# A pooling mixer with two-level fast products: output weights kept as split pairs in memory, and a second-level product for one more block

## The chip, the cores and the metric

The kernel runs on one core of one Trainium2 chip. The metric is the device time of one execution, in microseconds (us). The engines that matter are TensorE (matrix products; PE in the profile, its weight loads PEld), VectorE (DVE), ScalarE (ACT), GpSimd (POOL) and the DMA queues, which are fed by SyncE (SP) and by GpSimd.

## The reference

With DEPTH = 1 only the pooling mixer runs. For x of 4096 frames by 1024 channels, in float32:

```python
normed = rms_norm(x, norm_w)
u, gate = split(normed @ in_w, 2)              # in_w: 1024 x 2048
pooled = trailing_mean(u, 2 / 4 / 8 / 16 by channel group) - u
mixed = einsum('bsgc,gcd->bsgd', pooled, group_w) + group_b
y = mixed * scale * silu(gate)
h = x + y @ out_w                              # out_w: 1024 x 1024
out = rms_norm(h, final_norm_w)
```

## The kernel before, in words

Each product of matrices is computed in float32 precision from float32r operands: a value is stored as a high part (a copy to float32r on ScalarE) and a low part (value minus high part, a subtraction on VectorE), and a product is the sum of three matmuls, high times high, high times low and low times high (`mm3`, line 794). Writing the two parts is called splitting (`split`, line 203).

On top of this, products are made by a fast scheme with seven products P1 to P7 of half-size blocks in place of eight (a Strassen-Winograd scheme). Both sides need sums of their blocks first. In some places one of the seven is itself computed by seven smaller ones, which the code calls inner products.

The steps are a list, executed by one loop (line 1894 on): four input blocks of 1024 frames for the first side ("a", blocks a0 to a3), four for the second side ("b", b0 to b3; the gate and the rest of the pooled channels), each with the seven products in the order P1, P2, P7, P6, P5, P4, P3; then eight output blocks of 512 frames ("o", o0 to o7) in the order P1, P7, P6, P2, P5, P4, P3. A product of an input block is 48 matmuls of 512 columns, one of an output block 24. In b1 to b3 P7 is an inner product of 84 matmuls of 256 columns (`product_seven`, line 733). In the output blocks:

- o0: all seven products plain.
- o1: P2 as seven inner leaves of 6 matmuls of 256 columns each (`product_inner`, line 970; `leaf`, line 933). The leaves P2, P4, P1, P3, P7 run in the place of P2, the leaf P6 within the product P5, between its two rows, and the leaf P5 after it.
- o2 to o7: P2 as in o1 and P7 as an inner product as well, in an order written out by hand (`steady`, line 1511; from two steps ahead of o2 each engine's instructions keep the order of the program, class `InOrder`, line 65).

Up to there the order on each engine is chosen by the framework's scheduler, which goes by the order of the program and by when it thinks that an instruction's inputs are ready. `tc.issue_after(x)` puts instructions behind x on x's engine.

The inner product P2 needs sums of the four quarters of the weight's blocks (`sum_inner`, line 841, from two raw halves read by `load_inner`, line 836) and their splits (`split_weight`, line 864), which live in three of the `st` buffers ("kept") and in a quarter of P2's own weight tile, so the plain P2 can't be used once they are formed. In the kernel before they are formed during o0 and o1 (the table `forming`, line 1877). The operand's sums are made by `split_inner` (line 882), whose second half (`rest`, line 898) runs at the step P6. `add_inner` (line 981) adds a PSUM bank of the inner product into the rows of the output on VectorE; the leaf P6 writes a bank that the first of these additions reads.

Output weights: `load_wo` and `make_wo` (lines 376 and 381) run in b1 and b2 at P7 and P6, one half of out_w each: the rows are scaled on ScalarE, the sums of the blocks made on VectorE (`combine`, line 290), and the seven results stored to memory as float32 by SP's queue (`store_weights`, line 303; tensors `wod`). In b3 `load_w` (line 387) reads each back into a buffer on SP's queue, half by half (512 KB), and splits it into the weight tile `w`, as soon as the input side has used that tile for the last time.

Buffers: 11 tiles `st` and 8 tiles `vt` of 4 KB a partition, handed out in order of age (class `Slots`, line 37); a load into a buffer waits until its last user is done. Four tiles `op` hold split operands in turn (`next_op`, line 546). The pooled and gated result y is stored to memory (`yd`, function `pool`, line 1052) and read back by the output blocks. The residual x is added into the output rows by GpSimd's DMA (`add_h`, line 1162).

Of the kernel before, what the change touches and what calls it, by code (L numbers as in the profile page):

```python
# [15 lines left out]
P = 128  # L16
# [70 lines left out]
def kernel(  # L87
# [115 lines left out]
    def split(dst, src):  # L203
# [14 lines left out]
    t3d = [dram.tile([P, 2, H], F32, name=f"t3d{h}") for h in range(2)]  # L218
    wod = {
        i: [dram.tile([P, 2, H], F32, name=f"wod{i}_{h}") for h in range(2)]  # L220
        for i in range(P1, P7 + 1)
    }
    sd = [
        {
# [78 lines left out]
    def store_weights(dst, h, b11, b21, b12, b22):  # L303
        sync.dma_start(out=dst[P1][h], in_=b11)
        sync.dma_start(out=dst[P2][h], in_=b21)
        for i, u in combine(b11, b21, b12, b22).items():
            sync.dma_start(out=dst[i][h], in_=u)
            give(u)


# [75 lines left out]

    def load_w(src, i):
        for h in range(2):
            u = take()
            sync.dma_start(out=u, in_=src[i][h])  # L390
            with tc.issue_after(evicted[0]):
                split(w[i][h], u)
            give(u)
# [482 lines left out]
    def end_weights(i):  # L876
        for u in raws.pop(i)["held"]:
            give(u)
# [306 lines left out]

    def split_o(b, i):
        s = oxs[b]
        if i == P2 and b >= OWN - 1:
            return split_inner(s["12"])
        t = next_op("p (s a b) -> p s a b", s=2, a=4)  # L1190
        if i == P7:
            s["3"] = take("p (a b) -> p a b", a=4)
            sub(s["3"], s["11"], s["21"])
        elif i == P6:
            add(s["21"], s["21"], s["22"])
            sub(s["11"], s["21"], s["11"])
# [668 lines left out]
    def row_plan(b):  # L1865
# [8 lines left out]
        )  # L1874

    scales, summed = {}, []
    forming = {
        (0, P4): lambda: load_inner(P2),
        (0, P3): lambda: sum_inner(P2),
        (1, P1): lambda: split_weight(P2, P7, P6),  # L1880
        (1, P7): lambda: (split_weight(P2, P5, P4), end_weights(P2), load_inner(P7)),
        (1, P6): lambda: sum_inner(P7),
        (1, P4): lambda: (split_weight(P7, P7, P6, P5, P3), keep_temps(P7)),
    }
    forming_seven = (P7, P6, P5, P4)

    for n in range(2, len(steps)):
# [15 lines left out]
            for j in rows.get(i, ()):  # L1903
                load_row(b + 1, j // 4, j % 4, early if b == 0 and i == P7 else None)
        if kind == "o":
            while len(gathered) < (6 if b else 3 * (i in (P4, P3))) and st.free and len(st.free) + len(vt.free) > 4:
                gathered.append(st.keep())
                kept.append(gathered[-1])
# [8 lines left out]
        if kind == "o" and (b, i) in forming:  # L1917
            with tc.issue_after(latest_split[0]), tc.issue_after(latest_copy[0]):
                forming[b, i]()
        if n >= own_from - 2:  # L1920
            InOrder.on = n == own_from - 2 or InOrder.on
            steady(n)
# [44 lines left out]
        if kind in ("a", "b"):  # L1967
# [1 line left out]
            if kind == "a":  # L1969
                pool_due(n)  # L1970
            if kind == "b" and b == NB - 1:
                for p in {P1: (), P2: (), P7: (P1,), P6: (P2, P7), P5: (P6, P5)}.get(i, (i,)):
                    load_w(wod, p)
            if kind == "b" and b in (1, 2) and i == P7:
                load_wo(b - 1)
# [61 lines left out]
```

## Time and profile before

| | |
|---|---|
| median of 3 runs | 907.41 us (906.5 to 909.38) |
| profiled execution | 907.14 us, span of its instructions 905.3 us |
| TensorE busy | 894.6 us (99%), 4554 matmuls |
| VectorE busy | 736.8 us (81%) |
| ScalarE busy | 518.6 us (57%) |
| GpSimd busy | 147.3 us (16%) |
| granted TensorE clock | 0.998 of full speed |
| DMA | 203.30 MB, mean 225 GB/s |

How to read the lines below: a group of instructions is given by engine, operation, the tile written, the tiles read and their shapes, then the count, busy time in us and the mean duration of one in ns, then the idle time of the engine just before them with what ended it. In lists in order of time the first number is the start and the second the duration, both in us, with the idle time before it and its releaser in brackets. Nearly all elementwise work has the line L79, that of the recording helper, so one goes by tiles. L799 is the plain product (`mm3`), L941 the leaves of the inner P2 and of the inner P7 in the output blocks, L745 the inner P7 of the input blocks. A matmul's duration overlaps the next one's, so what a matmul costs is read from the distance of starts in a long stream. By the chain, P7 of b1 starts at 417.60 us; the plain products of o0 begin at 612.0 us.

### The profile page before, as it was taken

What the parts mean: (1) busy time and instruction counts of PE and PEld (TensorE: products, weight loads), DVE (VectorE), ACT (ScalarE), POOL (GpSimd) and SP (SyncE); (2) the same over time, 40 slices, a digit from 0 to 9 for tenths busy, and PEclk for the clock granted to TensorE, in tenths of its full rate; (3) what the DMA queues carried; (4) which work ended last, traced back from release to release, by engine and by line L of the source; (5) the groups of instructions that cost most, each with busy time, mean ns of one, the idle gap of its engine ahead of it and who ended that gap; (6) DMA issues with size and microseconds to landing.
All of it is one profiled execution on the core that took longest, in us unless ns stands there. A gap on an engine that the chain in (4) does not pass through costs nothing.

```text
span 905.3 us, 12421 instructions
## 1 busy us (share of the span) xinstructions
PE 894.6 (99%) x4554; PEld 791.7 (87%) x4554; DVE 736.8 (81%) x910; ACT 518.6 (57%) x848; POOL 147.3 (16%) x244
## 2 busy tenths in 40 slices
PE   9999999999999999999999999999999999999996
PEld 7888888888888888889889889888889898998996
DVE  3899896984996997694596497699898878888798
ACT  7869547446445465346545644855557466565464
POOL 0031110110111000100010011011132343342430
PEclk9999999999999999999999999999999999999999
DMA  9989779677769565245574574756673855945953
GB/s 339 402 313 320 263 279 314 219 299 286 270 248 363 180 236 183 94 163 190 212 244 175 202 262 142 269 188 204 206 220 81 221 176 142 240 143 138 264 179 116
DMA packets 77756, 203.30 MB, mean 225 GB/s; under 512 B 7296, under 2 KB 25088, under 8 KB 77696
## 3 DMA queue, kind: packets, MB, share of 16 engines
q1 hardware_dynamic: 57872, 143.77, 46.0%
q0 software_dynamic: 19104, 57.69, 20.7%
q10 hardware_dynamic: 720, 1.06, 0.3%
q8 instruction: 35, 0.57, 0.3%
q14 instruction: 25, 0.20, 0.1%
HBM read 130.13 MB, written 72.36 MB: 224 GB/s over the span
## 4 chain that ended last, share of the span: by engine, by line
PE 50%; DVE 21%; DMA 10%; issue 6%; ACT 3%; POOL 1%; SPq 0%; DVEq 0%; POOLq 0%; ACTq 0%
PE bank L799 44%; DVE vt L79 8%; DVE st L79 6%; DVE op L79 5%; PE bank L745 3%; DMA vt<-yd 3%; PE bank L941 3%; DMA st<-wvd 2%; ACT op L79 1%; DMA st<-yd 1%; DVE w L79 1%; DMA out<-vt 1%; ACT vt L79 1%; DMA st<-wod 1%; DMA vt<-rd 1%
## 5 line engine op out<-in xcount | busy, mean ns | idle before, releaser
L799 PE MATMUL bank<-op,w 128*128 128x512 f32 x2544 | 550.6, 379 | 0.2 <-ACT st L79 0.2
L799 PEld LDWEIGHTS bank<-op,w 128*128 128x128 f32 x2544 | 480.4, 189 | 68.9 <-ACT st L79 0.6
L799 PE MATMUL bank<-w,op 128*128 128x512 f32 (+1 forms) x1044 | 230.5, 377 | 0.0
L799 PEld LDWEIGHTS bank<-w,op 128*128 128x128 f32 x1044 | 192.3, 189 | 25.0
L79 DVE TENSOR_TENSOR op<-st,op 128x1024 fp32r<-128x1024 f32 x120 | 145.9, 1220 | 60.1 <-ACT op L79 59.7
L79 ACT ACTIVATE op<-st 128x1024 fp32r<-128x1024 f32 x120 | 125.8, 1052 | 86.4 <-PE bank L799 31.2
L79 ACT ACTIVATE op<-vt 128x1024 fp32r<-128x1024 f32 x65 | 68.3, 1053 | 63.0 <-DVE vt L79 40.6
L79 ACT ACTIVATE vt<-bank 128x512 f32<-128x512 f32 (+1 forms) x122 | 67.4, 577 | 43.9 <-PE bank L799 37.8
L79 DVE TENSOR_TENSOR op<-vt,op 128x1024 fp32r<-128x1024 f32 x65 | 78.4, 1218 | 14.2 <-ACT op L79 14.1
L79 DVE TENSOR_TENSOR st<-st,st 128x1024 f32<-128x1024 f32 (+1 forms) x47 | 51.3, 1104 | 31.6 <-ACT st L79 16.8
L79 ACT ACTIVATE bank<-bank 128x512 f32<-128x512 f32 (+1 forms) x84 | 41.1, 490 | 53.1 <-PE bank L799 39.5
L79 POOL COPY vt<-tails 128x32 f32<-128x32 f32 x14 | 17.0, 1219 | 301.4 <-ACT tails L79 130.3
L79 ACT ACTIVATE st<-bank 128x512 f32<-128x512 f32 (+1 forms) x62 | 35.6, 588 | 37.5 <-PE bank L799 22.7
L79 DVE TENSOR_TENSOR vt<-bank,vt 128x512 f32<-128x512 f32 (+1 forms) x90 | 51.3, 596 | 6.0 <-PE bank L941 4.6
L79 ACT ACTIVATE st<-st 128x1024 f32<-128x1024 f32 x34 | 35.8, 1055 | 28.6 <-DVE st L79 27.1
L79 DVE TENSOR_TENSOR st<-bank,st 128x512 f32<-128x512 f32 (+1 forms) x72 | 43.7, 622 | 6.0 <-PE bank L941 3.1
L79 POOL DMA_DIRECT2D sd<-st x45 | 24.0, 535 | 125.1 <-DVE st L79 77.9
L941 PEld LDWEIGHTS bank<-w,op 128*128 128x128 f32 x312 | 40.4, 191 | 1.7
L79 DVE TENSOR_TENSOR st<-st,vt 128x1024 f32<-128x1024 f32 (+1 forms) x34 | 39.1, 1168 | 2.7 <-DMA vt<-rd 2.4
L941 PE MATMUL bank<-w,op 128*128 128x256 f32 x312 | 41.1, 275 | 0.0
L79 DVE TENSOR_TENSOR vt<-vt 128x1024 f32<-128x1024 f32 (+3 forms) x43 | 38.2, 890 | 0.2
L79 DVE TENSOR_TENSOR_SCAN vt<-vt,window 128x1040 f32<-128x1040 f32 x16 | 37.7, 2374 | 0.6 <-DMA wod<-vt 0.5
(118 smaller groups left out, 768.5 us busy)
## 6 DMA issues: line engine op xcount, KB each, us to landing
sd<-st POOLq DMA_DIRECT2D x45, 512.0 KB, 4.2
st<-sd SPq DMA_DIRECT2D x42, 512.0 KB, 4.0
st<-in_xt SPq DMA_DIRECT2D x28, 512.0 KB, 7.4
st<-in_x SPq DMA_DIRECT2D x21, 512.0 KB, 7.9
yd<-st SPq DMA_DIRECT2D x20, 512.0 KB, 3.3
vt<-yd SPq DMA_DIRECT2D x17, 512.0 KB, 10.5
st<-wod SPq DMA_DIRECT2D x16, 512.0 KB, 5.1
out<-vt POOLq DMA_DIRECT2D x16, 512.0 KB, 3.5
```

The source lines that it names most:

```text
L79: r = f(*args, **kwargs)
L745: latest[0] = nc.tensor.matmul(cell(n, c).rearrange("p (a s) -> p a s", s=2), x1, x2, start=i == P1 and k + m == 0, stop=k == 1 and m == 2 ...
L799: latest[0] = nc.tensor.matmul(ps, a, b, start=start and n == 0, stop=stop and n == 2, skip_group_check=True).ins
L941: latest[0] = nc.tensor.matmul(ps, x1, x2, start=start and k + n == 0, stop=k == 1 and n == 2, skip_group_check=True,).ins
```

## The change

The sums for P5, P4 and P3 of the output weights are split where they are made, in b1 and b2: `store_weights` copies the high part into a second buffer, subtracts it, and stores both to new tensors `pair...` by SP's queue. In b3 (P5 and P4 at the steps P4 and P3, P3 at P3) `load_w` reads each half of a pair, 1 MB, straight into the weight tile by GpSimd's queue, with no buffer and no split. P1, P2, P6 and P7 are loaded and split as before.

P2 of o0 becomes an inner product like that of o1. Its weights are therefore formed earlier: loaded at P2 of b3, summed at P7, three `st` buffers taken at P6, split at P5 and P4. The weights of the inner P7 are formed in o1 as before.

```diff
     wod = {
         i: [dram.tile([P, 2, H], F32, name=f"wod{i}_{h}") for h in range(2)]
-        for i in range(P1, P7 + 1)
+        for i in (P1, P2, P6, P7)
+    }
+    pairs_d = {
+        i: [dram.tile([P, 2, 2, H], F32, name=f"pair{i}_{h}") for h in range(2)]
+        for i in (P5, P4, P3)
     }
...
         for i, u in combine(b11, b21, b12, b22).items():
-            sync.dma_start(out=dst[i][h], in_=u)
+            if i in dst:
+                sync.dma_start(out=dst[i][h], in_=u)
+            else:
+                high = take()
+                latest_copy[0] = copy(high.bitcast(F32R), u).ins
+                latest_split[0] = sub(u.bitcast(F32R), u, high).ins
+                for v, t in enumerate((high, u)):
+                    sync.dma_start(out=pairs_d[i][h][:, v], in_=t)
+                give(high)
             give(u)
...
     def load_w(src, i):
         for h in range(2):
+            if i not in src:
+                gpsimd.dma_start(out=w[i][h], in_=pairs_d[i][h].bitcast(F32R))
+                continue
             u = take()
             sync.dma_start(out=u, in_=src[i][h])
...
     def split_o(b, i):
         s = oxs[b]
-        if i == P2 and b >= OWN - 1:
+        if i == P2:
             return split_inner(s["12"])
...
+    def gather(count):
+        for _ in range(count):
+            gathered.append(st.keep())
+            kept.append(gathered[-1])
+
     forming = {
-        (0, P4): lambda: load_inner(P2),
-        (0, P3): lambda: sum_inner(P2),
-        (1, P1): lambda: split_weight(P2, P7, P6),
-        (1, P7): lambda: (split_weight(P2, P5, P4), end_weights(P2), load_inner(P7)),
-        (1, P6): lambda: sum_inner(P7),
-        (1, P4): lambda: (split_weight(P7, P7, P6, P5, P3), keep_temps(P7)),
+        ("b", NB - 1, P2): lambda: load_inner(P2),
+        ("b", NB - 1, P7): lambda: sum_inner(P2),
+        ("b", NB - 1, P6): lambda: gather(3),
+        ("b", NB - 1, P5): lambda: split_weight(P2, P7, P6),
+        ("b", NB - 1, P4): lambda: (split_weight(P2, P5, P4), end_weights(P2)),
+        ("o", 1, P7): lambda: load_inner(P7),
+        ("o", 1, P6): lambda: sum_inner(P7),
+        ("o", 1, P4): lambda: (split_weight(P7, P7, P6, P5, P3), keep_temps(P7)),
     }
...
-                for p in {P1: (), P2: (), P7: (P1,), P6: (P2, P7), P5: (P6, P5)}.get(i, (i,)):
+                for p in {P1: (), P2: (), P7: (P1,), P6: (P2, P7), P5: (P6,), P4: (P5,), P3: (P4, P3)}[i]:
                     load_w(wod, p)
```

More of the change, by code (lines that the diff above doesn't have):

```diff
@@ L1905 @@
         if kind == "o":
-            while len(gathered) < (6 if b else 3 * (i in (P4, P3))) and st.free and len(st.free) + len(vt.free) > 4:
-                gathered.append(st.keep())
-                kept.append(gathered[-1])
+            while b and len(gathered) < 6 and st.free and len(st.free) + len(vt.free) > 4:
+                gather(1)
             if b > 0 or i in (P4, P3):
@@ L1916 @@
             advance("split", n, split_step, split_reach)
-        if kind == "o" and (b, i) in forming:
+        if (kind, b, i) in forming:
             with tc.issue_after(latest_split[0]), tc.issue_after(latest_copy[0]):
-                forming[b, i]()
+                forming[kind, b, i]()
         if n >= own_from - 2:
```

## The prediction

> **What bounds the kernel now.** I read the busy times first, then the time cut into stages, then the chain that ended last, and then, around the one place where TensorE stops, its instructions and VectorE's in order of time. The page's head:
>
> ```profile
> span 905.3 us, 12421 instructions
> PE 894.6 (99%) x4554; PEld 791.7 (87%) x4554; DVE 736.8 (81%) x910; ACT 518.6 (57%) x848; POOL 147.3 (16%) x244
> ```
>
> TensorE lacks 10.7 us of the span. The table by stages says where (start:end; TensorE, weight loads, VectorE, ScalarE, GpSimd busy with their counts; granted clock; DMA share; GB/s):
>
> ```profile
> 660.00:670.00 10.00, 9.91 (x61) 8.76 (x59) 9.93 (x14) 8.20 (x13) 4.34 (x6) 1.00 0.86 239
> 670.00:680.00 10.00, 8.31 (x44) 7.49 (x45) 9.99 (x18) 2.42 (x4) 1.77 (x2) 1.00 0.96 252
> 850.00:906.00 56.00, 48.01 (x278) 43.42 (x276) 46.86 (x93) 27.40 (x59) 11.62 (x19) 0.96 0.54 167
> ```
>
> Some 8 us are the last stage, 56.00 less 48.01, of which 0.7 lie past the end; the change touches nothing there. Between 660 and 680 are 0.09 + 1.69 us, the only gap that the change can close; the rest is the start. So it can gain only by issuing less TensorE work or by closing that gap. The gap, in order of time on TensorE:
>
> ```profile
> 612.01 51.96 PE L799 MATMUL bank<-w,op 128*128 128x512 f32 x240
> 667.16 2.76 PE L799 MATMUL bank<-w,op 128*128 128x512 f32 x12
> 671.69 0.94 PE L941 MATMUL bank<-inner,op 128*128 128x256 f32 x6 [1.77 <-DVE vt L79]
> ```
>
> The 240 are ten products of 24: all seven of output block 0 (612.0 to 648.4) and three of block 1. At 671.69 the inner product P6 of block 1 starts 1.77 us late. Its bank is read first by an addition on VectorE, which in the order of its queue stands behind this:
>
> ```profile
> 666.29 0.68 DVE L79 TENSOR_TENSOR vt<-vt 128x512 f32<-128x512 f32 x1
> 667.01 1.42 DVE L79 TENSOR_TENSOR vt<-vt,vt 128x512 f32<-128x512 f32 x2
> 668.94 2.35 DVE L79 TENSOR_TENSOR op<-vt,op 128x1024 fp32r<-128x1024 f32 x2
> 671.22 0.42 DVE L79 TENSOR_TENSOR vt<-bank,vt 128x256 f32<-128x256 f32 x1
> ```
>
> VectorE is simply behind there. How long it has been shows in the stages:
>
> ```profile
> 443.00:486.00 43.00, 43.00 (x201) 37.65 (x200) 42.42 (x46) 18.04 (x26) 3.69 (x4) 1.00 0.65 225
> 514.00:558.00 44.00, 44.00 (x206) 38.53 (x205) 41.75 (x44) 18.90 (x27) 4.50 (x3) 1.00 0.60 210
> 587.00:640.00 53.00, 53.00 (x247) 46.43 (x246) 52.83 (x53) 26.15 (x34) 9.39 (x8) 1.00 0.69 210
> 640.00:671.00 31.00, 29.91 (x154) 26.27 (x152) 27.46 (x36) 22.47 (x42) 8.95 (x20) 1.00 0.58 183
> ```
>
> From 587 to 640 it is busy 52.83 of 53 us, from 640 to 671 27.46 of 31.
>
> **The change, part by part.** First TensorE. Block 0's P2 loses 24 matmuls of 512 columns and gets seven leaves of 6 of 256 columns, 42. Both kinds stand in the chain in undisturbed streams:
>
> ```profile
> 427.20 62.16 PE bank L799 x288
> ...
> 701.29 3.35 PE bank L941 x30
> ```
>
> 62.16/288 = 0.2158 us and 3.35/30 = 0.1117 us. 24 x 0.2158 = 5.18 less 42 x 0.1117 = 4.69: 0.49 us gained, with no cover, since TensorE is the bound. The Trainium skill (TensorE: Matmul & The Clock Gate, Back-to-back issue gap) speaks against it: it gives 131 ns for a sustained 512-column matmul and 81 ns for 128 columns, since the weight load has its share; about halfway in columns, an estimate of 97 ns for 256, the swap would cost 42 x 97 - 24 x 131 ns = 0.9 us. The rows here show 216 and 112 ns, so the measurement decides.
>
> Then the elementwise work that moves:
>
> ```profile
> L79 DVE TENSOR_TENSOR w<-st,w 128x1024 fp32r<-128x1024 f32 x25 | 29.6, 1218 | 5.5 <-ACT w L79 5.5
> L79 ACT ACTIVATE w<-st 128x1024 fp32r<-128x1024 f32 x25 | 25.5, 1054 | 6.0 <-DVE st L79 2.4 <-DMA st<-wod 2.1 <-PE bank L799 1.4
> L79 DVE TENSOR_TENSOR inner<-vt,inner 128x512 fp32r<-128x512 f32 x6 | 3.9, 679 | 0.0
> L79 ACT ACTIVATE inner<-vt 128x512 fp32r<-128x512 f32 x6 | 3.6, 633 | 0.0
> L79 DVE TENSOR_TENSOR vt<-bank,vt 128x256 f32<-128x256 f32 x29 | 11.4, 416 | 4.7 <-PE bank L941 4.6
> ```
>
> Splits of P5, P4, P3: six copies of 1.05 and six subtractions of 1.22 us leave input block 3 and the start of output block 0 (7.3 us of VectorE, 6.3 of ScalarE) and go, three each, to P6/P5 of input blocks 1 and 2 of the second side: 3.7 us of VectorE and 3.2 of ScalarE in each. VectorE is full after both (42.42 of 43, 41.75 of 44), so all behind them comes later. What waits is the split of operands, four tiles ahead of TensorE:
>
> ```profile
> 443.13 1.23 DVE L79 TENSOR_TENSOR st<-st,st 128x1024 f32<-128x1024 f32 x1 [8.39 <-ACT st L79]
> 451.21 1.21 DVE L79 TENSOR_TENSOR op<-st,op 128x1024 fp32r<-128x1024 f32 x1
> 452.34 1.21 DVE L79 TENSOR_TENSOR op<-vt,op 128x1024 fp32r<-128x1024 f32 x1
> 447.96 1.06 ACT L79 ACTIVATE op<-vt 128x1024 fp32r<-128x1024 f32 x1 [2.97 <-PE bank L799]
> ```
>
> The copy at 447.96 waits for the tile that P5 has just left, so it fills the fourth tile ahead, and the subtraction at 451.21 belongs to the third: P3's first half. With 48 matmuls a product (10.36 us) from 427.20, P3 starts at 458.3, the subtraction ends at 452.4: 5.9 us of cover. Starts 1.13 us apart make the three added ones 3.4 us, so 2.5 are left. Cost nothing; without the cover 3.4 us in each block. The same holds for the three stores more in SP's queue of each block (seven become ten): loads of later operands stand behind them and come up to 3.4 us later, plus 1.5 MB of traffic at 225 GB/s, 7 us at the very worst; I take none of it, and both ends go to the range.
>
> What is left of this backlog reaches the inner P7 of block 3, where cover is thin:
>
> ```profile
> 560.46 0.17 DVE L79 TENSOR_REDUCE window<-vt 128x1 f32<-128x16 f32 x1 [2.43 <-POOL vt L79]
> 562.74 1.23 DVE L79 TENSOR_TENSOR op<-st,op 128x1024 fp32r<-128x1024 f32 x1 [0.98 <-ACT op L79]
> 564.31 0.83 PE L745 MATMUL bank<-op,w 128*128 128x256 f32 x6
> ```
>
> The subtraction at 562.74 ends at 564.0 and feeds the matmuls of 564.31. Of 3.4 us late, 2.43 and 0.98 go into these two waits if they shrink; if the first is passed on (GpSimd waits there for a store that itself follows VectorE), about 0.8 us are lost. I take none.
>
> Inner weights of P2: four half-size sums and four splits of 0.68 us (5.4 us of VectorE, 2.5 of ScalarE) and two loads of 512 KB move from output blocks 0 and 1 to P2 to P4 of input block 3. New for block 0: four sums of about 0.42 (1.7), a second split (1.22 and 1.05), six additions of 0.42 (2.5): 5.4 us of VectorE. Balance from 587 on: -7.3 + 2.7 (the splits of the weights; the sums fall before) + 2.9 = -1.7 by block 0's P2; the additions bring +2.5, and 5.4 are gone after 640: some 4.6 us less before 671. That is more than the 1.77 of the gap. But GpSimd's read-and-add of x into these rows moves one product later in block 0, its squares later still, and ScalarE waits for them in order: up to 3 us come back. I take 1.5 of the 1.78 as gained; bounds 0 and 1.78.
>
> The loads of P5, P4, P3 become six of 1 MB on GpSimd's queue, without a buffer in between. Each waits until TensorE has left that half of the old weights (586.1, 591.3, 596.5, 601.6, 606.8, 612.0, half a product apart), and GpSimd's copies of window history and its adds of x are queued behind. They are due at P5 (632.8), P4 (638.0) and P3 (643.2). DMA has room then:
>
> ```profile
> 604.00:619.00 15.00, 15.00 (x71) 13.12 (x71) 15.00 (x13) 9.08 (x13) 0.00 (x0) 1.00 0.15 57
> 624.00:641.00 17.00, 17.00 (x81) 14.88 (x80) 16.13 (x16) 5.34 (x8) 4.02 (x5) 1.00 1.08 302
> ...
> sd<-st POOLq DMA_DIRECT2D x45, 512.0 KB, 4.2
> ...
> st<-in_x POOLq DMA_DIRECT2D x18, 256.0 KB, 7.5
> ```
>
> No row shows 1 MB, nor a load that writes float32r. By the plain store it is at most 2 x 4.2 = 8.4 us; by the adding load 4 x 7.5 = 30 us. I take the plain one, as these only move data. One after another from 586.1 the last lands at 636.5, 7 us ahead: cost nothing.
>
> **Sum.** -0.49 - 1.5 = -2.0 us. The profiled execution took 907.14 us around its span of 905.3, and the median of the three is 907.41, so it stands 0.27 lower. 907.14 - 2.0 = 905.2 us (0.24% under the median). The most that all terms can give is -0.49 - 1.78: 904.9.
>
> **The rivals.**
> Slow pair loads (slower). If a megabyte on GpSimd's queue takes over (643.2 + 1.3 - 586.1)/6 = 9.7 us, P3's second half is late, and from there each us costs six: at 12 us it lands at 658, 14 us late, 919 us. For it: the adding load's 7.5 us for a quarter of the size. Against: that one was measured where DMA was full (1.08), these run where it is 0.15. The Trainium skill (DMA: Bandwidth & Descriptors, SWDGE vs HWDGE vs iDMA) says that a DMA into float32r always casts and must be issued from GpSimd; no run here shows what such a cast takes.
>
> Buffers (slower). Two buffers hold P2's halves and three its sums through input block 3, 5 of 19 (11 + 8). SP gets loads off at the pace at which buffers come free:
>
> ```profile
> 571.26 1.41 SPq L79 DMA_DIRECT2D st<-sd  x2
> 583.96 8.92 SPq L79 DMA_DIRECT2D st<-wod  x6
> ```
>
> 8.92/6 = 1.5 us each, so five fewer are 7.4 us late loads. Operands loaded at 571.26 serve products from 591.3 on, which covers that; from about 12 us on TensorE waits, and each further us counts: 3 to 6 us, 908 to 911. Against: six loads for splits take no buffer any more.
>
> The gap stays, or moves to block 0, where the same bank now has the same reader: 907.14 - 0.49 = 906.7, with both 908.4. For it: VectorE is full there as well; against: the balance above.
>
> The backlog at block 3's P7: 905.2 + 0.8 = 906.0.
>
> Short matmuls paced by their weight loads: from 5.18/42 = 0.123 us each the swap loses; at 0.146 it is 1 us worse than nothing, 906.6. The row of 0.1117 speaks against it. It is the rule of the skill's page named above.
>
> **How the numbers follow.** Covers hold: 0.55, 905.2, by its own range 904.5 to 906.5. Gap stays or moves: 0.14. Backlog: 0.05. Matmul pace: 0.03. Buffers: 0.11. Slow pair loads: 0.12. What this kernel's measurement can tell from no change is about 0.3%, 2.7 us: under 904.7 or over 910.1. Faster by more needs the likeliest case with all of its terms and a little luck: 0.17 of its 0.55. Slower: buffers and pair loads, 0.23. The rest, 0.60, is within. The range runs from 904.2 to 912.0; outside are most of the slow pair loads, the far end of the buffers and a little below.
>
> **What would show it.** Right: 42 more short and 24 fewer long matmuls; no idle TensorE near 670; VectorE with idle time between 612 and 671; six 1 MB loads landing under 9.7 us each, and the copies of P3's weights gone from ScalarE near 613. Wrong: TensorE waiting for a DMA into w in block 0, for a split in input blocks 1 to 3, or for an addition from a bank near 633.

## The result and the profile after

The changed kernel takes 929.49 us (median of 4 runs, 927.58 to 930.88) against 906.95 for the kernel before in the same session: a ratio of 1.0235 (95% interval 1.0213 to 1.0257). It is 2.35% slower; 905.2 was predicted, with 912.0 as the upper end. Of the runs further down, one of the four of held_late took 4430 us and is left out of its median.

The profiled execution took 927.58 us. Its head, with busy times by engine:

```profile
span 925.8 us, 12489 instructions
...
PE 902.2 (97%) x4572; PEld 797.3 (86%) x4572; DVE 743.0 (80%) x921; ACT 518.5 (56%) x849; POOL 150.0 (16%) x250
```

The span grew by 20.5 us in two parts. TensorE's idle time is 925.8 - 902.2 = 23.6 us, where it was 10.7: 12.9 more. And TensorE is busy 7.6 us longer, though its work shrank by the 0.49 us of the swap (4572 matmuls, 18 more, as 42 less 24 say). The idle part, in order of time on TensorE (start, duration, what runs, and in brackets the wait before it with its releaser; lines are 15 further down than before, so L814, L956 and L760 are the former L799, L941 and L745):

```profile
470.24 2.00 PE L814 MATMUL bank<-op,w 128*128 128x512 f32 x8 [1.22 <-DVE op L79]
475.06 22.04 PE L814 MATMUL bank<-op,w 128*128 128x512 f32 x87 [2.82 <-DVE op L79]
576.38 1.37 PE L760 MATMUL bank<-op,inner 128*128 128x256 f32 x6 [4.84 <-ACT st L79]
641.90 2.86 PE L814 MATMUL bank<-w,op 128*128 128x512 f32 x12 [2.31 <-ACT bank L79]
652.17 3.92 PE L814 MATMUL bank<-w,op 128*128 128x512 f32 x10 [3.63 <-DVE op L79]
```

The gap near 670 is gone, as predicted. In its place are five waits, 14.82 us together, at three places: the first product of b2 (1.22 + 2.82), the inner P7 of b3 (4.84), and o0 at its P6 and P5 (2.31, 3.63).

The longer busy time has its row in the table by stages (start:end; length, TensorE, weight loads, VectorE, ScalarE, GpSimd; then granted clock, DMA share, GB/s), just behind the wait of 2.82 us:

```profile
475.00:480.00 5.00, 4.95 (x12) 3.96 (x13) 5.00 (x7) 1.07 (x2) 0.00 (x0) 0.50 0.82 275
```

Twelve matmuls in 5 us, at half the clock; 22.04/87 = 0.253 us a matmul over the whole stretch, against 0.2158. Behind the wait in b3 the clock is 0.67 from 575 to 580, behind the one at 652 it is 0.68 for 5 us. In all the slower clock takes 7.6 + 0.49 = 8.1 us beside 14.82 us of waits.

At the first two places, what the instructions wait for leads to buffers, at the third to VectorE. ScalarE, at each of the three:

```profile
455.46 1.06 ACT L79 ACTIVATE st<-st 128x1024 fp32r<-128x1024 f32 x1 [2.55 <-DMA pair<-st]
572.63 1.08 ACT L79 ACTIVATE st<-bank 128x512 f32<-128x512 f32 x2 [5.73 <-DMA yd<-st]
640.30 1.06 ACT L79 ACTIVATE op<-st 128x1024 fp32r<-128x1024 f32 x1 [5.33 <-DVE st L79]
```

The first copies the high part of a pair into a buffer that is still being stored as another pair. The second empties a bank of b3 into a buffer that is still being stored as y. Both stand in an ordered queue, with TensorE's operands or banks behind them. The third is in o0: the copy of the operand for a later product waits for VectorE, which is busy with hardly a gap from 626.65 on, and the copy of a bank that TensorE needs at 641.90 stands behind it.

The suspect that the prediction had priced the highest is quiet. The six megabyte loads land at a median of 7.1 us:

```profile
w<-pair POOLq DMA_DIRECT2D x6, 1024.0 KB, 7.1
```

### The profile page after: what moved, and what is told of

Its sections match the earlier page's. It is cut to its first block, busy times and chain, and to the rows that moved or that the text cites. A ratio compares the mean times of both kernels' runs of the same rounds, so it can differ in the third digit from the quotient of the medians.

```text
span 925.8 us, 12489 instructions
## 1 busy us (share of the span) xinstructions
PE 902.2 (97%) x4572; PEld 797.3 (86%) x4572; DVE 743.0 (80%) x921; ACT 518.5 (56%) x849; POOL 150.0 (16%) x250
## 4 chain that ended last, share of the span: by engine, by line
PE 71%; DVE 12%; DMA 8%; issue 4%; ACT 3%; POOL 0%; DVEq 0%; SPq 0%; ACTq 0%; POOLq 0%
PE bank L814 60%; DVE vt L79 5%; PE bank L956 5%; DVE op L79 3%; DVE st L79 3%; PE bank L466 3%; PE bank L760 3%; DMA st<-wod 2%; ACT st L79 1%; DMA vt<-yd 1%; DMA st<-sd 1%; DMA st<-wvd 1%; ACT op L79 1%; DMA st<-yd 1%; ACT vt L79 1%
## 5 line engine op out<-in xcount | busy, mean ns | idle before, releaser
L814 PE MATMUL bank<-op,w 128*128 128x512 f32 x2544 | 554.2, 381 | 4.1 <-DVE op L79 4.0
L814 PEld LDWEIGHTS bank<-op,w 128*128 128x128 f32 x2544 | 482.2, 190 | 74.5 <-DVE op L79 4.8
L814 PE MATMUL bank<-w,op 128*128 128x512 f32 (+1 forms) x1020 | 227.8, 379 | 5.9 <-DVE op L79 3.6
L814 PEld LDWEIGHTS bank<-w,op 128*128 128x128 f32 x1020 | 188.4, 190 | 31.2 <-DVE op L79 4.0
L79 ACT ACTIVATE vt<-bank 128x512 f32<-128x512 f32 (+1 forms) x119 | 65.2, 574 | 36.3 <-PE bank L814 29.1
L79 DVE TENSOR_TENSOR st<-st,st 128x1024 f32<-128x1024 f32 (+3 forms) x46 | 48.6, 1073 | 29.8 <-ACT st L79 16.8
L79 ACT ACTIVATE st<-st 128x1024 f32<-128x1024 f32 (+1 forms) x38 | 40.0, 1056 | 33.0 <-DVE st L79 28.1
L79 DVE TENSOR_TENSOR st<-bank,st 128x512 f32<-128x512 f32 (+1 forms) x85 | 48.2, 586 | 5.0 <-DMA st<-in_x 2.9
L79 DVE TENSOR_TENSOR st<-st,vt 128x1024 f32<-128x1024 f32 (+1 forms) x37 | 42.8, 1173 | 3.1 <-DMA vt<-rd 3.0
L956 PEld LDWEIGHTS bank<-w,op 128*128 128x128 f32 x336 | 43.4, 191 | 1.8
L956 PE MATMUL bank<-w,op 128*128 128x256 f32 x336 | 44.3, 275 | 0.0
```

The source lines that it names most:

```text
L79: r = f(*args, **kwargs)
L814: latest[0] = nc.tensor.matmul(ps, a, b, start=start and n == 0, stop=stop and n == 2, skip_group_check=True).ins
L956: latest[0] = nc.tensor.matmul(ps, x1, x2, start=start and k + n == 0, stop=k == 1 and n == 2, skip_group_check=True,).ins
```

## The experiments

The theories, as the expectations name or use them: A, work moved earlier takes buffers from the stages that it is moved into, or queues behind its neighbours there; B, the 1 MB loads on GpSimd's queue; C, the inner P2 of o0 by itself. Within A, for the pairs: D1, the second buffer of each split; D2, the added VectorE and ScalarE work. The kernel before took 907.2 to 907.9 us beside these runs.

| run | what it is | us | ratio to before (95%) |
|---|---|---|---|
| pairs_only | pairs alone | 912.40 | 1.0055 (1.0035 to 1.0075) |
| pairs_unsplit | its sums stored twice, not split | 905.86 | 0.9984 (0.9972 to 0.9996) |
| pairs_in_place | its splits without a second buffer | 906.76 | 0.9989 (0.9978 to 1.0000) |
| pairs_gp_store | its stores on GpSimd's queue | 912.63 | 1.0054 (1.0032 to 1.0076) |
| pairs_p3 | pairs for P3 alone | 907.98 | 1.0010 (0.9996 to 1.0025) |
| pairs_earlier | pairs one step earlier | 909.70 | 1.0022 (1.0010 to 1.0034) |
| pairs_later, again as pairs_later_5 | pairs one step later | 906.51, 906.89 | 0.9990, 0.9991 (0.9981 to 1.0002) |
| inner_only | inner P2 in o0 alone | 917.11 | 1.0103 (1.0080 to 1.0125) |
| held_buffers | before, five buffers held | 920.55 | 1.0140 (1.0106 to 1.0174) |
| held_two | two of the five | 912.38 | 1.0056 (1.0043 to 1.0069) |
| held_three | the other three | 908.85 | 1.0017 (1.0006 to 1.0029) |
| held_late, again as held_late_2 | the five, three steps later | 915.74, 917.68 | 1.0093, 1.0110 (1.0083 to 1.0137) |
| late_forming | the change, weights formed three steps later | 920.27 | 1.0131 (1.0107 to 1.0155) |
| late_gp_store | that, pair stores on GpSimd's queue | 922.82 | 1.0164 (1.0142 to 1.0186) |
| late_unsummed | late_forming without o0's sums | 918.49 | 1.0125 (1.0111 to 1.0138) |
| late_both | late_forming, pairs one step later | 914.60 | 1.0078 (1.0059 to 1.0097) |

### The two halves of the change, each alone

pairs_only keeps the pairs and their loads, and leaves o0's P2 plain with its weights formed as before:

```diff
 # the kernel before, with the change's hunks in wod / pairs_d,
 # store_weights, load_w and the table of load_w's steps, and no other
```

> Only the first half of the change: P5, P4, P3 stored as pairs, P2 of output block 0 plain and its inner weights formed in o0 and o1 as before. Theory A (the sums and splits that come earlier lack buffers and queue up behind each other, and each half of the change pays at its own place): the two waits of TensorE at P1 of input block b2 stay (4.0 us in the changed kernel, some 7 with the slower clock behind them), the waits at P7 of b3 and in o0 go; some 910 to 914 us. Theory B (the 1 MB loads on GpSimd's queue): waits in o0 stay, some 917 us. Theory C (the inner P2 of o0 alone is to blame): no waits, 905 to 907 us.

inner_only keeps `if i == P2: return split_inner(...)` and the new table `forming`, and loads and splits P5, P4, P3 as before:

```diff
-        if i == P2 and b >= OWN - 1:
+        if i == P2:
...
-        (0, P4): lambda: load_inner(P2),
+        ("b", NB - 1, P2): lambda: load_inner(P2),
 # and so on, as in the change; load_w as before
```

> Only the second half: P2 of output block 0 inner, its weights formed in b3 with five buffers held there, while P5, P4, P3 are loaded and split in b3 as before. Theory A: the waits at P7 of b3 (4.8 us in the changed kernel) and in o0 (2.3 + 3.6 us) stay or grow, since the loads of P5, P4, P3 now want buffers too; some 918 to 930 us; none at b2. Theory B: no waits, 906 us. Theory C: as A at this run, 918 us or more.

Each half loses: 5.2 and 9.9 us. TensorE's waits are those of the changed kernel, shared out. First pairs_only:

```profile
469.34 1.99 PE L814 MATMUL bank<-op,w 128*128 128x512 f32 x8 [1.22 <-DVE op L79]
474.15 20.73 PE L814 MATMUL bank<-op,w 128*128 128x512 f32 x87 [2.82 <-DVE op L79]
```

and inner_only:

```profile
566.62 1.65 PE L745 MATMUL bank<-op,inner 128*128 128x256 f32 x6 [3.44 <-ACT st L79]
630.53 2.07 PE L799 MATMUL bank<-w,op 128*128 128x512 f32 x4 [2.25 <-ACT op L79]
634.01 6.22 PE L799 MATMUL bank<-w,op 128*128 128x512 f32 x20 [1.40 <-DVE op L79]
```

The pairs make the waits in b2, the inner product those in b3 and o0. In pairs_only the gap near 670 shrank to 0.31 us. In inner_only, which splits P5, P4 and P3 in b3 as before, it is gone as well, but there TensorE comes to that place some 10 us later, so the changed kernel alone can't tell what closed it. All six megabyte loads are in pairs_only, with no wait for them, so B falls; and as the pairs lose without the inner product, C falls as the whole cause.

### The pairs: what makes TensorE wait in b2

pairs_unsplit takes the copy, the subtraction and the second buffer away; pairs_in_place keeps all twelve instructions and takes only the second buffer away:

```diff
 # pairs_unsplit, in store_weights
-                high = take()
-                latest_copy[0] = copy(high.bitcast(F32R), u).ins
-                latest_split[0] = sub(u.bitcast(F32R), u, high).ins
-                for v, t in enumerate((high, u)):
-                    sync.dma_start(out=pairs_d[i][h][:, v], in_=t)
-                give(high)
+                for v in range(2):
+                    sync.dma_start(out=pairs_d[i][h][:, v], in_=u)
```

> pairs_only without the splits in b1 and b2: the same twelve 512 KB stores from SP and the same six 1 MB loads on GpSimd's queue, but no copy of the high part, no subtraction and no second buffer (the sum is stored twice, so the low parts are wrong). If the stores and loads cost (SP's queue, DMA): as pairs_only, with its waits at P1 of b2. If the splits and their buffers cost: 4 us or more under pairs_only, no wait at b2, 905 to 907 us, and by then also less wait near 670.

```diff
 # pairs_in_place, at the same place
+                latest_copy[0] = copy(u, u).ins
+                latest_split[0] = sub(u.bitcast(F32R), u, u).ins
+                for v in range(2):
+                    sync.dma_start(out=pairs_d[i][h][:, v], in_=u)
```

> pairs_only with the same six copies and six subtractions and the same stores in b1 and b2, but each done in place, so that no second buffer is wanted (the low parts come out as zero: the pair stands for another number and the output is wrong). pairs_only waits 4.0 us at P1 of b2 (912.4 us), pairs_unsplit not at all (905.9 us). Theory D1 (the second buffer: the next copy waits until the last pair's store has landed, and operand loads queue up behind): no wait at b2, 905 to 907 us. Theory D2 (3.4 us more of VectorE and 3.2 of ScalarE in each of two blocks, whose VectorE is full): the wait stays, 910 to 912 us.

In pairs_in_place TensorE has one wait between 300 and 885 us, what is left of the old gap:

```profile
669.84 0.94 PE L954 MATMUL bank<-inner,op 128*128 128x256 f32 x6 [0.37 <-DVE vt L79]
```

The same VectorE and ScalarE work and the same stores cost nothing (906.76, and 905.86 without the work, intervals that overlap). D2 falls, D1 is shown: the 5.2 us are those of the second buffer. In b2, where the same three buffers are taken, no wait of TensorE follows; why was not followed further.

pairs_gp_store asks whether the order of SP's queue, loads behind the added stores, is the way in which the buffer acts:

```diff
                 for v, t in enumerate((high, u)):
-                    sync.dma_start(out=pairs_d[i][h][:, v], in_=t)
+                    gpsimd.dma_start(out=pairs_d[i][h][:, v], in_=t)
```

> pairs_only with one edit: the twelve stores of pairs go by GpSimd's queue, which is idle in b1 and b2, and not by SP's, where the loads of later operands stand behind them. The second buffer stays. If the operand loads were late because they stood behind these stores in SP's queue: no wait at P1 of b2, 905 to 907 us. If the loads were late for want of buffers, or VectorE was: the wait stays at 2.5 us or more, 910 to 912 us.

It changes nothing in the time (912.63), but it moves the waits. SP's waits between 444 and 476 us (total, times, longest) show that with no pair store in its queue, its loads still wait for the pairs' stores to land, since they go into those buffers. TensorE:

```profile
SPq L79 <- DMA pair<-st: 12.9, 3, 7.5
...
470.54 0.48 PE L814 MATMUL bank<-op,w 128*128 128x512 f32 x1 [0.98 <-ACT op L79]
471.80 19.48 PE L814 MATMUL bank<-op,w 128*128 128x512 f32 x89 [0.78 <-DVE op L79]
568.22 0.94 PE L760 MATMUL bank<-op,inner 128*128 128x256 f32 x6 [2.38 <-ACT st L79]
```

In b2 4.04 us of waits have become 1.76, so the order of SP's queue does carry part of them. In their place 2.38 us stand at the inner P7 of b3, where pairs_only has none: there ScalarE's eviction, its copy of a bank into a buffer, waits 2.82 us, since that buffer is still being stored as y. Why it does so with this edit was not followed.

pairs_p3 lowers the count of second buffers in a block from three to one:

```diff
-        for i in range(P1, P7 + 1)
+        for i in (P1, P2, P6, P7, P5, P4)
+    }
+    pairs_d = {
+        i: [dram.tile([P, 2, 2, H], F32, name=f"pair{i}_{h}") for h in range(2)]
+        for i in (P3,)
```

> The kernel before with P3 alone stored as a pair: one second buffer in each of b1 and b2 in place of three, two 1 MB loads in place of six. With three the waits at P1 of b2 were 1.22 and 2.82 us (912.4 us); with none (the same copies and subtractions in place) there was no wait and the gap near 670 fell from 1.8 to 0.4 us (0.9989 of before). If it is the count of second buffers, one in place of three waits under 1 us at P1 of b2, and the gap near 670 keeps part of its length, as a third of the splits has moved: 906 to 907.5, ratio 0.999 to 1.001. If any second buffer at that place is too much, the wait at b2 is 2 to 4 us: 910 to 912.

The wait in b2 is gone, and so is the gain: the gap near 670 is 2.33 us in this profile, and the time can't be told from before. So one second buffer in a block makes no wait where three do, and a third of the splits moved gains nothing.

pairs_earlier and pairs_later move all three pairs by one step:

```diff
 # pairs_later (pairs_earlier: P2 and P7)
-            if kind == "b" and b in (1, 2) and i == P7:
+            if kind == "b" and b in (1, 2) and i == P6:
                 load_wo(b - 1)
-            if kind == "b" and b in (1, 2) and i == P6:
+            if kind == "b" and b in (1, 2) and i == P5:
```

> pairs_only with the raw rows loaded at P2 and the sums and pairs made at P7, one step earlier, in b1 and b2. If the wait at P1 of b2 is set by how close before it the second buffers are taken, 10 us more let their stores land, the wait goes and the time is 905.5 to 907. If buffers are as short at P7, whose sums take some themselves, the wait moves into P7 to P5 of the same block or stays: 909 to 914.

> pairs_only with the raw rows loaded at P6 and the sums and pairs made at P5, one step later. If the wait is set by the distance to b2's loads, it grows past the 4.0 us of pairs_only: 914 to 918. If it is set by the buffers that P7's sums hold, which have come back by then, it goes: 905.5 to 907.

> The kernel of pairs_later in more rounds, beside before: 0.998 to 1.000 if the gap near 670 that it shortened by 0.8 us is all that it gains, 1.000 to 1.001 if the single look flattered it. No wait between 440 and 480 in either case.

Moved earlier, the wait in b2 goes, but four smaller ones stand in b1 and b2 (0.63, 0.50, 0.63, 0.50 us). Moved later, there is no wait at all between 300 us and the old gap:

```profile
671.11 0.94 PE L956 MATMUL bank<-inner,op 128*128 128x256 f32 x6 [0.60 <-DVE vt L79]
```

That line is of pairs_later_5; ScalarE's copy into the buffer of an earlier pair waits 0.75 us in pairs_later, 2.63 in pairs_only. The wait is one of place, not of pairs as such. Why the step P5 has more buffers to spare than P6 was not followed further. At 0.9991 (0.9981 to 1.0002) this is the best that the change's parts gave, no slower than before, and not shown to be faster.

### The inner product: buffers or work

held_buffers moves no work. It only takes the five buffers out of use that the new table `forming` takes, at the same steps:

```diff
+    held_back = []
+    holding = {
+        ("b", NB - 1, P2): lambda: held_back.extend(take() for _ in range(2)),
+        ("b", NB - 1, P6): lambda: gather(3),
+        ("b", NB - 1, P4): lambda: [give(u) for u in held_back],
+    }
...
+        if (kind, b, i) in holding:
+            holding[kind, b, i]()
```

> The kernel before with the buffers alone: two buffers are taken at P2 of b3 and given back at P4, and the three kept ones are taken at P6 of b3, and nothing is read into or written to any of the five until the kernel before would have done so; no work is moved or added. If the lack of buffers is enough (theory A in its narrow form): loads come late and TensorE waits in b3 or o0, 912 to 925 us. If it is the added work on VectorE and ScalarE: 907 us.

It is the strongest single result: 13.4 us lost with nothing computed otherwise. But it is not yet the share of the buffers in the change: this kernel still forms the weights of P2 in o0 and o1 as before, with two more buffers there, and inner_only, which holds the five and does the work, lost 9.9 beside it. What makes the 3.4 us between them was not followed. TensorE, then ScalarE at the first of these waits, then SP's queue:

```profile
567.30 1.32 PE L745 MATMUL bank<-op,inner 128*128 128x256 f32 x6 [2.80 <-ACT st L79]
634.55 44.17 PE L799 MATMUL bank<-w,op 128*128 128x512 f32 x192 [6.62 <-ACT op L79]
...
563.55 1.09 ACT L79 ACTIVATE st<-bank 128x512 f32<-128x512 f32 x2 [3.68 <-DMA yd<-st]
...
592.76 23.33 SPq L79 DMA_DIRECT2D st<-wod  x7
```

The wait in b3 has the same cause as in the changed kernel: an eviction into a buffer not yet stored. The wait in o0 comes by another way. The loads of output weights take 23.33 us for seven, 3.3 each, where the prediction quoted 8.92 for six, 1.5 each. VectorE, which splits what they bring, falls behind. Before:

```profile
560.00:600.00 40.00, 40.00 (x227) 36.14 (x226) 29.42 (x30) 29.04 (x41) 4.24 (x3) 1.00 0.76 254
600.00:640.00 40.00, 40.00 (x187) 35.04 (x186) 39.83 (x39) 18.32 (x24) 5.37 (x6) 1.00 0.63 188
```

and with five buffers held:

```profile
560.00:600.00 40.00, 37.20 (x205) 33.74 (x204) 20.83 (x21) 23.67 (x35) 1.03 (x2) 0.96 0.53 181
600.00:640.00 40.00, 33.38 (x144) 28.22 (x143) 39.99 (x39) 19.38 (x25) 2.98 (x4) 0.91 0.61 183
```

VectorE does 8.6 us less between 560 and 600 (20.83 against 29.42), and from 600 to 640, where it is full in both, there is no room to make it up. Its last splits of weights that were read back start 10.5 us later than before, though TensorE, from its wait in b3, comes to o0 only 5.4 us later (617.40 against 612.01). The kernel before, then five held:

```profile
617.22 2.35 DVE L79 TENSOR_TENSOR w<-st,w 128x1024 fp32r<-128x1024 f32 x2
...
627.67 2.33 DVE L79 TENSOR_TENSOR w<-st,w 128x1024 fp32r<-128x1024 f32 x2
```

That is how, in this run, late loads become a wait of TensorE 40 us on.

held_two and held_three part the five:

```diff
 # held_two leaves out of held_buffers:
-        ("b", NB - 1, P6): lambda: gather(3),
 # held_three leaves out the two other entries
```

> The kernel before with two buffers taken out of use from P2 to P4 of b3, and nothing else (the three kept ones are taken in o0 as before). With both groups out of use TensorE waited 2.80 us at P7 of b3 and 6.62 in o0, 920.6 us. If the two make the wait at P7 of b3 alone, 2.5 to 4 us stay there and o0 has none: 910 to 913. If the two also set off o0's wait (loads that come late in a row), 916 to 920. If one group alone is harmless, within 1 us of before.

> The kernel before with the three kept buffers taken at P6 of b3 in place of P4 of o0, and nothing else. If these three make o0's wait, 5 to 7 us of it stay and P7 of b3 has none: 913 to 916. If o0's wait comes from the two others or only from all five together, within 1 us to 3 us of before: 907 to 910.

The two cost 5.0 us, the three 1.5; all five 13.4, twice the sum. Neither group alone makes a wait in o0: what two make is 1.30 us in b3 and 2.84 in place of 1.77 at the gap in o1, so the time of held_two is the one expected, its waits are not. So the price of a held buffer rises with their number, which no balance of the busy times had shown.

held_late holds five at the steps of late_forming, the run after it, P5 and P3 of b3:

```diff
-        ("b", NB - 1, P2): lambda: held_back.extend(take() for _ in range(2)),
-        ("b", NB - 1, P6): lambda: gather(3),
-        ("b", NB - 1, P4): lambda: [give(u) for u in held_back],
+        ("b", NB - 1, P5): lambda: held_back.extend(take() for _ in range(2)),
+        ("b", NB - 1, P3): lambda: gather(3),
+        ("o", 0, P7): lambda: [give(u) for u in held_back],
```

> The kernel before with two buffers out of use from P5 of b3 to P7 of o0 and the three kept ones taken at P3 of b3: the buffers of late_forming, held at its steps, and no work moved or added. late_forming took 920.3 us, of which the pairs make some 4 at P1 of b2, the inner product's work in o0 or these buffers the rest. If the buffers make the waits of o0, 4 to 8 us of waits appear between 600 and 680 and the time is 911 to 917. If it is the work, at most the 1.8 us of before near 670 stay and the time is 907 to 909.

> The kernel of held_late once more, for a profile in which the waits can be read: 914 to 918 us. If the buffers alone delay loads, VectorE does less than the 29.4 us of before between 560 and 600 us, its work is pushed into o0 and o1, and TensorE's waits between 600 and 690 sum to 8 to 11 us (before: 1.8). If the waits lie elsewhere, the theory of late loads falls.

The lines are those of held_late_2. The wait in b3 is gone, those in output blocks 0 and 1 are not. TensorE, then ScalarE at the first of them:

```profile
639.23 31.77 PE L799 MATMUL bank<-w,op 128*128 128x512 f32 x132 [3.57 <-ACT st L79]
679.74 1.65 PE L941 MATMUL bank<-inner,op 128*128 128x256 f32 x6 [2.80 <-DVE st L79]
...
638.10 1.08 ACT L79 ACTIVATE st<-bank 128x512 f32<-128x512 f32 x2 [6.98 <-DMA yd<-st]
```

The two sum to 6.4 us, where 8 to 11 were expected; the remainder of the loss is again the clock, 31.77/132 = 0.241 us a matmul after the first. And the first is not the wait of held_buffers in o0: it is once more an eviction into a buffer that is still being stored as y. VectorE did 28.04 us between 560 and 600, 1.4 less than before, and 35.52 from 600 to 640, 4.3 less: here it isn't full ahead of the wait. So the buffers cost 8 to 10 us at these steps too, but late loads, the theory of the expectation, don't make the wait in o0.

late_forming gives the changed kernel those steps:

```diff
-        ("b", NB - 1, P2): lambda: load_inner(P2),
-        ("b", NB - 1, P7): lambda: sum_inner(P2),
-        ("b", NB - 1, P6): lambda: gather(3),
-        ("b", NB - 1, P5): lambda: split_weight(P2, P7, P6),
-        ("b", NB - 1, P4): lambda: (split_weight(P2, P5, P4), end_weights(P2)),
+        ("b", NB - 1, P5): lambda: load_inner(P2),
+        ("b", NB - 1, P4): lambda: sum_inner(P2),
+        ("b", NB - 1, P3): lambda: gather(3),
+        ("o", 0, P1): lambda: split_weight(P2, P7, P6),
+        ("o", 0, P7): lambda: (split_weight(P2, P5, P4), end_weights(P2)),
```

> The changed kernel with the inner weights of P2 formed later: halves loaded at P5 of b3, summed at P4, three buffers kept from P3, splits at P1 and P7 of o0. So two buffers are held from P5 of b3 to P7 of o0 and three from P3 on, in place of P2 to P4 and P6 on. If the buffers held early cause the wait at P7 of b3 (4.8 us) this wait goes; the waits in o0 (2.3 + 3.6) shrink if they follow from loads that came late in b3, and stay or grow if they follow from the inner product's own work on VectorE in o0. The wait at b2 (4.0) stays. Some 914 to 920 us against 929.5.

late_gp_store adds the diff of pairs_gp_store to it:

> late_forming and the pairs stored by GpSimd's queue, the two mends together. If SP's queue and the early buffers were all: 905 to 908 us, with the waits at b2 and at P7 of b3 gone. Otherwise the waits that are left show what else there is.

late_forming wins back 9.2 of the 22.5 us. The wait in b3 falls from 4.84 to 0.37 us, the one in b2 stays (1.22 + 2.74), and o0 keeps two of 3.06 and 3.03. GpSimd's queue for the stores moves the waits here too and gains nothing: b2 keeps 1.99 of 3.96 us, b3 has 2.68 in place of 0.37, and the time is 922.82, with intervals that overlap.

late_unsummed asks whether the two in o0 are the inner product's own work, by leaving its sums, their split and its additions out for o0:

```diff
 # split_inner, when b == 0: no v, no second split
+            for i in (P7, P6, P5, P3):
+                t[i] = t[P1]
+            return t
 # add_inner, for that block
+            return
```

> late_forming with the leaves of o0's inner P2 kept on TensorE, but without the four sums of its operand, their split and the six additions of the inner bank into the rows (5.4 us of VectorE, 1.1 of ScalarE and one buffer for a short time; the leaves multiply plain quarters instead of sums and their bank is never added, so this block's output is another one). In late_forming TensorE waits in o0 for 3.06 us on a split operand and for 3.03 on the split before it. If the added VectorE and ScalarE work in o0 makes these waits, both shrink to under 1 us and the time falls by 4 to 7 us, to 913 to 916. If the buffers held through the start of o0 make them (operands that are read back late), they stay within 1 us of their length and the time stays at 918 to 921. The wait of 2.74 us in b2 stays in both.

Neither expectation held. The waits in o0 go, and the time falls by 1.8 us at most (0.5 by the ratios, whose intervals overlap), since others take their place in o1. On TensorE, then on VectorE:

```profile
666.02 5.45 PE L814 MATMUL bank<-w,op 128*128 128x512 f32 x24 [1.85 <-ACT bank L79]
674.61 0.71 PE L961 MATMUL bank<-w,op 128*128 128x256 f32 x4 [0.81 <-DVE op L79]
681.00 0.94 PE L961 MATMUL bank<-inner,op 128*128 128x256 f32 x6 [2.42 <-DVE vt L79]
...
651.56 1.23 DVE L79 TENSOR_TENSOR st<-st,st 128x1024 f32<-128x1024 f32 x1 [6.95 <-issue]
```

The 4.7 us of VectorE that were spared (737.7 us busy in place of 742.4) are idled away at once: 6.95 us in front of a subtraction for o1 (the profile names no releaser; SP issued a load of y at 640.98, and such loads land after a median of 10.5 us in this stretch, which points to it but doesn't show it). So the work decides where TensorE waits, and hardly how long: 5.08 us in o1 in place of 6.09 in o0. That points to the buffers, which cost 8 to 10 us by themselves in held_late, but doesn't show them to be the cause in o0: of held_late's two waits the first has another reason, and the second is in o1. How the waits in o0 divide between the held buffers and the product's own work stays open.

late_both puts the two better places together, late_forming and the pairs of pairs_later:

> late_forming with the pairs made one step later as in pairs_later: both fixes of place at once, all of the change's work kept. If the wait at P1 of b2 and the waits in o0 are separate costs, the former's 4 us go and 915 to 917 are left, what the held buffers cost with no work. If they are linked (a later o0 gets less behind when b2 is not late), 909 to 913. If the pairs' later place delays the forming, 918 to 921.

914.60, between two of the cases expected. No wait in b2 or b3, two in o0:

```profile
634.04 2.43 PE L814 MATMUL bank<-w,op 128*128 128x512 f32 x10 [2.66 <-DVE op L79]
640.55 1.65 PE L956 MATMUL bank<-inner,op 128*128 128x256 f32 x6 [4.09 <-DVE st L79]
```

This gives the loss as a sum of steps, each a pair of runs. The medians are of different sessions, in which the kernel before differed by up to 1.0 us, and in another order the steps could come out otherwise. Before to pairs at a better place: -0.7 us (906.89 against 907.55). The inner product with weights formed late: +7.7 (914.60). The pairs back at the change's step: +5.7 (920.27). The forming back at its step: +9.2 (929.49). Open stays why late_both, with work and buffers, is 1 to 3 us faster than held_late with the buffers alone, as inner_only is 3.4 us faster than held_buffers.

## Why the prediction was wrong

**The swap on TensorE, -0.49.** Right in its mechanism and its count (18 more matmuls). In late_unsummed, where o0's leaves ran undisturbed, two groups of six start 0.67 us apart, 0.112 us each, the price that was used (the estimate of 97 ns for 256 columns beside it was taken a third of the way from 128 to 512 columns, not halfway, and decided nothing):

```profile
633.16 0.83 PE L961 MATMUL bank<-w,op 128*128 128x256 f32 x6
633.83 0.83 PE L961 MATMUL bank<-inner,op 128*128 128x256 f32 x6
```

**The gap near 670, -1.5.** Right as far as pairs_in_place shows: with the splits of P5, P4 and P3 and their loads through buffers away from b3 and o0, 0.37 of 1.77 us is left. Whether the splits close it, as the balance of VectorE had it, or the loads, was not parted. That the gap is gone in the changed kernel shows less, as inner_only has lost it too. Without the second buffer, or at the better step, the pairs are worth 0.7 to 1.3 us, at the edge of what these runs can tell.

**"Cost nothing": the splits in b1 and b2.** This is the first step that failed. It weighed three subtractions of 1.13 us against a cover of 5.9 at P3, and there it held: P3 doesn't wait, and the same work in place costs nothing. What the step left out is one line of the diff, `high = take()`: three more buffers in each block, each out of use until its store has landed. The waits came one product later, at the start of b2, where the prediction had not looked, though a wait for a split in input blocks 1 to 3 was among its signs of being wrong. The step costs 5.2 us, with what closing the gap gains taken off.

**"I take none": the loads behind the added stores.** The bounds, 3.4 to 7 us, held the cost, but for a reason that is a part of it only. With the stores out of SP's queue (pairs_gp_store) the waits in b2 fall from 4.04 to 1.76 us and the time stays; with no second buffer (pairs_in_place) and the same stores in the queue there is no wait. It is the buffers that the stores and the loads go through.

**The inner P7 of b3, +0.8 as a rival.** The place was right, the cause was not: not VectorE's backlog but an eviction that waits for a buffer. It cost 4.84 us of wait.

**The rival "Buffers", 3 to 6 us at a chance of 0.11.** This had the mechanism, and is the term that was mis-sized. Its working took 1.5 us for each of five missing buffers as one delay of 7.4 us, and set that against 20 us of cover for operands loaded ahead. Held alone in the kernel before, these five cost 13.4 us; held and used, in inner_only, 9.9. Three things were missing. In held_buffers a missing buffer delays each load again, 3.3 us in place of 1.5, not once. Evictions and splits take buffers as well as loads, and the evictions that wait in b3 and the copies that wait in b1 had no cover. And VectorE's idle time in b3, 10.6 of 40 us, was taken as spare; in held_buffers the loads came too late to use it, and o0, where VectorE is full, paid. "Against: six loads for splits take no buffer any more" weighed later steps: the loads of P5, P4 and P3 followed P6 of b3, and the first wait stands at P7.

**The balance of VectorE, -4.6 before 671.** As a sum of work it was right. As a forecast of where VectorE stands it was not: in the changed kernel it does 25.21 us from 560 to 600 and 34.01 from 600 to 640, where it did 29.42 and 39.83, and TensorE waits for it all the same. Less work doesn't help an engine whose inputs come late: at 626.65 it has stood 3.13 us for a load of y.

**Slow pair loads.** Refuted as expected: 5.1 to 8.8 us, so the longest is over the 8.4 taken from the plain store, and all are below the 9.7 from which they decide. No product waits for one.

**The clock.** No term had it: some 8 of the 20.5 us are TensorE working slower behind its waits.

The range ended at 912.0 because buffers were priced at 6 us at most, and because each part was priced alone: the halves of the change cost 15.1 us apart and 22.5 together.

## What to carry to other kernels

Count a change's buffers before its instructions: list what each stage holds, until which store or which reader, and where the pool is already handed out as fast as it comes back, price a held buffer by a run that holds it and moves nothing else. Such a run is a dozen lines, and it told more here than any balance of busy times, though not the buffer's exact share in the change. Where an engine is idle ahead of a stage in which it is full, that idle time may be its reserve against late inputs; work moved there is not free. And where TensorE is the bound, as here, count a wait of some 3 us at more than its length: in the changed kernel 14.8 us of waits came with 8.1 us of slower clock.

## What was not expected of the hardware

The granted clock behind a wait. After 2.82 us (pairs_only and the changed kernel) it fell to between 0.50 and 0.71 over the next 5 us, after 3.06 us in late_forming likewise (a second wait, of 3.03 us, lies in this row):

```profile
640.00:650.00 10.00, 6.97 (x20) 5.31 (x20) 7.28 (x11) 1.15 (x2) 0.00 (x0) 0.51 1.03 351
```

Behind waits of 1.77 (before), 2.33 (pairs_p3) and 2.74 us (late_forming at b2) it stayed at 1.00:

```profile
475.00:480.00 5.00, 5.00 (x25) 4.39 (x24) 5.00 (x8) 1.16 (x2) 0.00 (x0) 1.00 0.91 311
```

Behind every wait of 2.80 us or more in the traces from 300 to 885 us it fell. Below that there is no sharp edge: 2.31 (the changed kernel), 2.64 (late_unsummed) and 2.66 us (late_both) left it at 1.00 as well, while 2.25 (inner_only, 0.55), 2.38 (pairs_gp_store, 0.71), 2.62 and 2.68 us (late_gp_store, 0.66 and 0.69) did not, nor did 1.84 us with a wait of 1.01 shortly before it (held_three, 0.66). What decides between them was not followed. The Trainium skill (TensorE: Matmul & The Clock Gate, Part 1: The HAM clock gate) says that TensorE drops to half its clock after an idle window of about 3.4 us and needs about as long to come back. The half agrees with the 0.50 of the row at 475; the waits that set it off here are shorter than that window.
